# A hybrid DeltaNet and convolution block on one core: results in PSUM emptied by one engine each, and a 31-tap convolution that begins and ends in SBUF

## The chip, the core and the metric

The kernel runs on one core of a Trainium2 chip. The metric is the device time of one execution in microseconds (us). The core's engines, as the profile names them: PE (TensorE, matrix products; PEld is its loading of weights), DVE (VectorE), ACT (ScalarE), POOL (GpSimd) and SP (which here only issues DMAs). Each works through its own list of instructions in order and waits at semaphores for the others. Products land in PSUM, which PE writes and DVE and ACT read; everything else lies in SBUF.

## The reference

One layer, x of 512 tokens by 1024 channels, all in float32:

```python
h = rmsnorm(x, norm1_w)
q, k, v, z, b, a, glu, gates = split(h @ w_in)
q, k, v = silu(causal_depthwise_conv(q | k | v, 4 taps))        # 8 heads of 128
o = gated_delta_rule(l2norm(q), l2norm(k), v, decay(a), sigmoid(b))   # per head, in time
out_a = (rmsnorm(o) * silu(z)) @ dn_w_o
c = glu_a * sigmoid(glu_b)
c = causal_depthwise_conv(c, 31 taps) + cm_dw_b                 # 1024 channels
c = silu(layernorm(c))
out_b = c @ cm_w_pw2 + cm_b_pw2
x = x + (sigmoid(gate_a) * out_a + sigmoid(gate_b) * out_b) @ w_out
x = x + (silu(f_gate) * f_up) @ ffn_w_down                      # f_gate, f_up from rmsnorm(x)
return rmsnorm(x, norm_f_w)
```

The delta rule is S_t = a_t S_(t-1) (I - b_t k_t k_t^T) + b_t k_t v_t^T with o_t = q_t S_t. In chunks it needs the inverse of a unit lower triangular matrix per head and chunk.

## The kernel before

**Products.** Channels lie on the 128 partitions and the 512 tokens along the free axis. Each weight tile (128 x 1024, `raw`) is split into a high part on ACT (`whi`, L111) and a low part on DVE (`wlo`, L112), and a product in full precision is three matmuls: high by high, high by low, low by high (L121). One unit of weights is 24 such matmuls. The weights are loaded three units deep. PE works on these products from beginning to end; everything else is woven between them.

**The mixers**, up to some 475 us of the profile, is the stage that the change touches. A list of generators (`queue`) yields after every three matmuls, and each such step counts one. Besides the products of the projections three other things run there:

- The eight heads' delta rule. `chain(h, ...)` is a generator that says after each piece how many steps are to pass before the next. It builds the inverse of the triangular matrix of 128 x 128 in blocks of 16, 32 and 64: each `group(w, ...)` (L526) is two products into the single PSUM buffer `b`, whose results ACT and DVE carry to their places in `m64`, `Y` (the inverse) and `st64` (shown as `s`). DVE transposes 32 x 32 blocks as it carries them. Then come four state steps, n = 0 to 3, one per 128 tokens, in the single PSUM buffer `st`, which has four slots: slot 0 for k by the state (L622) and later for kd by `w` (L633), slot 2 for q by the state (L623), slot 1 for the inverse by `R` (L628), slot 3 for `at` by `w` (L634). ACT carries slot 1 out as `w` (L630). DVE makes the next state `S` from slot 0 (L640) and the output `o` from slot 3 and from `Ae`, which is slot 2 scaled (L646 and L647; `Ae` lies in a tile named `R`).
- The 31-tap convolution `conv31(i, c)`, eight tiles of 128 channels. ACT makes the first tap into the PSUM tile `cps` (L688), DVE adds 30 more there, one instruction each (L690), ACT copies the result to `cv[i]` in SBUF (L692), and DVE adds it to the running sum `sacc` (L696).
- The four-tap convolutions, the GLU and the gates.

After the last gate PE begins with the output projection of the heads (`yh`, `yl`, split at L878 and L879), and after its first unit of weights PE sums `sacc` over channels for the mean of the layer norm (L709).

**What sets the order.** The kernel is recorded in program order, and a scheduler then orders each engine's instructions by priorities and by its own idea of their times; after that the order is fixed. The taps of `conv31` are recorded with a lower priority (`OFF` = 1600), so they fill the gaps that the scheduler sees on DVE. The chains' steps are pinned behind what was issued last (`behind()`). Where ACT and DVE both read one PSUM buffer, semaphores let them take turns in program order. A product into that buffer waits for the last reader.

Of the kernel before, what the change touches and what calls it, by code (L numbers as in the profile page):

```python
# [6 lines left out]
F32 = mybir.dt.float32  # L7
F32R = mybir.dt.float32r
I32 = mybir.dt.int32
AF = mybir.ActivationFunctionType  # L10
ALU = mybir.AluOpType
# [3 lines left out]
P = 128  # L15
T = 512
# [16 lines left out]
def block_kernel(ctx, tc, a):  # L33
    nc = tc.nc
    V, S, G, PE = nc.vector, nc.scalar, nc.gpsimd, nc.tensor
# [23 lines left out]
    dw_b, ln_w, ln_b, b_pw2 = vec[:, 48:56], vec[:, 56:64], vec[:, 64:72], vec[:, 72:80]  # L59
# [3 lines left out]
    c31w = small.tile([P, KD, 31], F32, name="c31w")  # L63
# [69 lines left out]
    cv = [kp.tile([P, T], F32, name="cv", bufs=KD) for _ in range(KD)]  # L133
# [78 lines left out]
    with tc.tile_pool(name="st", bufs=2) as st:  # L212
# [56 lines left out]
        for k in range(KD):  # L269
# [3 lines left out]
                                   op0=ALU.mult, op1=ALU.subtract)  # L273
            if k % 2 == 0:
                c = slice(k * P, k * P + 256)
# [15 lines left out]
        ps = psg.tile([P, 4, P], F32, name="g")  # L291
# [50 lines left out]
        for k in range(2, 4):  # L342
# [6 lines left out]
                        in1=ss[:, 1].rearrange("p (n a) -> p n a", a=1).broadcast_to([P, NT, 16]), op=ALU.mult)  # L349
# [3 lines left out]
        beta, nbeta, kdf, egc, negc, egl, nmc = (sm[:, i] for i in range(7))  # L353
        ax, t0, sp, u, g, eb = (swt[:, 32 * i:32 * i + 32].rearrange("p (n h) -> p n h", n=NT) for i in range(6))
        V.tensor_tensor(out=ax, in0=bas[:, :, 8:16],
                        in1=rowp[:, 1:2, :].broadcast_to([P, NT, H]), op=ALU.add)
# [172 lines left out]
    def chain(h, kT, qT, ss, kd, b2, Un, cp, Vp, at, yq, zs):  # L529
# [62 lines left out]
            S.copy(out=Y[b, :, b], in_=YY[b])  # L592
        yield 4
        ps = group(32, st32[1], Q)
        S.copy(out=m64[b32[1], :, b32[0]], in_=ps[b32[1]])
        V.transpose(out=m64[b32[3], :, b32[0]], in_=ps[b32[0]])
        S.copy(out=Y[b32[2], od, b32[3]], in_=ps[b32[2]])
        V.transpose(out=Y[b32[2], ev, b32[3]], in_=ps[b32[3]])
        S.copy(out=Y[b32[0], od, b32[1]], in_=ps[b32[0]])
        V.transpose(out=Y[b32[0], ev, b32[1]], in_=ps[b32[1]])  # L600
        S.copy(out=Y[lo64, ev, hi64], in_=Y[hi64, od, hi64])
        yield 5

        ps = group(64, st64[0], m64)
        S.activation(st64[1][hi64, :, hi64], ps[hi64], AF.Copy)
        V.tensor_copy(out=st64[1][lo64, :, lo64], in_=ps[lo64])
        yield 4
        ps = group(64, st64[1], Y[:, ev, hi64])
        S.activation(Y[lo64, ev, hi64], ps[hi64], AF.Copy)
        V.tensor_copy(out=Y[lo64, od, hi64], in_=ps[lo64])  # L610
        yield 3

# [3 lines left out]
        for n in range(NT):  # L616

            ps = pst.tile([P, 4, P], F32, name="st")
            if n == 0:
                R = Vp[:, 0, :]  # L620
            else:
                PE.matmul(ps[:, 0, :], kT[:, n, :], Sp, start=True, stop=True)  # L622
                PE.matmul(ps[:, 2, :], qT[:, n, :], Sp, start=True, stop=True)  # L623
                R = gp.tile([P, P], F32, name="R", bufs=3)
                V.scalar_tensor_tensor(out=R, in0=ps[:, 0, :], scalar=negc[:, n, h:h + 1], in1=Vp[:, n, :],
                                       op0=ALU.mult, op1=ALU.add)
                yield 3
            PE.matmul(ps[:, 1, :], Y[:, n % 2 * 2 + n // 2, :], R, start=True, stop=True)  # L628
            w = gp.tile([P, P], F32, name="w", bufs=2)
            S.activation(w, ps[:, 1, :], AF.Copy, scale=b2[:, n:n + 1])  # L630
            yield 3
            if n < NT - 1:
                PE.matmul(ps[:, 0, :], kd[:, n, :], w, start=True, stop=True)  # L633
            PE.matmul(ps[:, 3, :], at[:, n, :], w, start=True, stop=True)  # L634
            if n < NT - 1:
                Sn = gp.tile([P, P], F32, name="S", bufs=2)
                if n == 0:
                    V.tensor_copy(out=Sn, in_=ps[:, 0, :])
                else:
                    V.scalar_tensor_tensor(out=Sn, in0=Sp, scalar=egl[:, n, h:h + 1], in1=ps[:, 0, :],  # L640
                                           op0=ALU.mult, op1=ALU.add)
            if n == 0:
                V.tensor_copy(out=o[:, 0, :], in_=ps[:, 3, :])
            else:
                Ae = gp.tile([P, P], F32, name="R", bufs=3)
                S.activation(Ae, ps[:, 2, :], AF.Copy, scale=egc[:, n, h:h + 1])  # L646
                V.tensor_tensor(out=o[:, n, :], in0=ps[:, 3, :], in1=Ae, op=ALU.add)  # L647
            S.activation(sq, o[:, n, :], AF.Square, accum_out=ss[:, 2, n:n + 1])
            if n < NT - 1:
                Sp = Sn  # L650
                yield 3
# [33 lines left out]

    def conv31(i, c):
        acc = psc.tile([P, T], F32, name="cps")
        S.activation(acc, c[:, 0:T], AF.Identity, scale=c31w[:, i, 0:1], bias=dw_b[:, i:i + 1])  # L688
        for k in range(1, 31):
            V.scalar_tensor_tensor(out=acc, in0=c[:, k:k + T], scalar=c31w[:, i, k:k + 1], in1=acc,  # L690
                                   op0=ALU.mult, op1=ALU.add)
        S.activation(cv[i], acc, AF.Copy)  # L692
        if i == 1:
            V.tensor_tensor(out=sacc, in0=cv[0], in1=cv[1], op=ALU.add)
        elif i > 1:
            V.tensor_tensor(out=sacc, in0=sacc, in1=cv[i], op=ALU.add)  # L696
# [690 lines left out]
```

## Time and profile before

| what | value |
|---|---|
| median of three runs | 951.15 us (949.65 to 952.15) |
| the profiled execution | 953.04 us, of which the span of the profile is 951.3 us |
| granted PE clock, mean | 0.997 |
| PE busy | 928.8 us, 98% of the span |
| DVE busy | 740.5 us, 78% |
| ACT busy | 560.8 us, 59% |
| POOL busy | 330.7 us, 35% |

A row of the waits' view reads "engine, tile and line <- what ended the wait: total us, times, longest us". A row of a timeline reads "start us, duration us, engine, line, operation, out<-in, shapes, count [idle time before it <- what ended it]". A row of the grouped view has the count, then busy us and mean ns of one, then the idle time before the group and what ended it. The rows of a table by stretches have the stretch, its length, the busy time of PE, PEld, DVE, ACT and POOL with counts, the granted clock, the DMA engines' share and GB/s. Numbers after tile names are left out there (`m<-b` is `m64`, `s` is one of `st16`, `st32`, `st64`).

### The profile page before, as it was taken

How to read it: one execution, taken by the hardware profiler on the slowest of the kernel's cores; microseconds unless marked ns; L12 is line 12 of the kernel's file. 1: busy time of each engine (PE TensorE's matmuls, PEld its weight loads, DVE VectorE, ACT ScalarE, POOL GpSimd, SP SyncE). 2: the span in 40 equal slices, each digit the busy share in tenths (PEclk: the TensorE clock that was granted, in tenths of full speed). 3: DMA queues.
4: the chain of work that ended last, by engine and by line, in shares of the span. 5: the costliest groups of instructions: out<-in, count | busy, mean ns of one | idle time of the engine just before them, and what ended most of it. 6: DMA issues, size and time to landing. Idle time of an engine off the chain costs nothing.

```text
span 951.3 us, 14518 instructions
## 1 busy us (share of the span) xinstructions
PE 928.8 (98%) x4952; PEld 785.9 (83%) x4952; DVE 740.5 (78%) x1157; ACT 560.8 (59%) x1277; POOL 330.7 (35%) x541
## 2 busy tenths in 40 slices
PE   9999999999999999999899999999999999999996
PEld 6778787878887888788778888888889999988885
DVE  4899598888888889899988643676636877888896
ACT  6698887878778786634447323333334454556545
POOL 0045524243443437544034350254441111133042
PEclk9999999999999999999999999999999999999999
DMA  9333322222222236998988983598898555567654
GB/s 321 110 134 104 122 90 78 99 92 68 84 90 87 99 135 148 312 280 268 283 274 253 274 255 131 174 290 285 279 251 233 174 188 187 178 220 253 226 182 150
DMA packets 78187, 177.39 MB, mean 186 GB/s; under 512 B 10080, under 2 KB 19472, under 8 KB 77088
## 3 DMA queue, kind: packets, MB, share of 16 engines
q1 hardware_dynamic: 66528, 144.89, 44.4%
q0 software_dynamic: 10288, 28.90, 13.1%
q10 hardware_dynamic: 1296, 2.67, 0.7%
q8 instruction: 39, 0.64, 0.3%
q14 instruction: 36, 0.29, 0.1%
HBM read 156.22 MB, written 45.37 MB: 212 GB/s over the span
## 4 chain that ended last, share of the span: by engine, by line
PE 70%; ACT 12%; DVE 6%; issue 3%; POOL 3%; DMA 1%; SPq 0%; POOLq 0%; ACTq 0%; DVEq 0%
PE mm L121 44%; PE w L121 20%; ACT whi L111 1%; DVE wlo L112 1%; PE b L526 1%; DVE cps L690 1%; DVE acc L422 1%; DMA sgd<-sg 1%; ACT Y L592 1%; ACT s L583 1%; ACT Un L473 1%; PE g L435 1%; ACT R L646 0%; PE st L628 0%; POOL y L504 0%
## 5 line engine op out<-in xcount | busy, mean ns | idle before, releaser
L111 ACT ACTIVATE whi<-raw 128x1024 fp32r<-128x1024 f32 (+1 forms) x191 | 196.6, 1030 | 250.5 <-PE mm L121 163.6
L112 DVE TENSOR_TENSOR wlo<-raw,whi 128x1024 fp32r<-128x1024 f32 (+1 forms) x191 | 238.0, 1246 | 82.0 <-ACT whi L111 80.2
L121 PE MATMUL mm<-hh,whi 128*128 128x512 f32 (+1 forms) x688 | 268.7, 391 | 0.3 <-ACT hh L336 0.3
L121 PE MATMUL mm<-hl,whi 128*128 128x512 f32 (+1 forms) x688 | 263.3, 383 | 0.0
L121 PE MATMUL mm<-hh,wlo 128*128 128x512 f32 (+1 forms) x688 | 263.1, 383 | 0.0
L690 DVE SCALAR_TENSOR_TENSOR cps<-c,c31w,cps 128x512 f32<-128x512 f32 x240 | 179.8, 749 | 4.2 <-ACT cps L688 0.5
L121 PEld LDWEIGHTS mm<-hh,wlo 128*128 128x128 f32 x688 | 129.6, 188 | 23.2
L121 PEld LDWEIGHTS mm<-hh,whi 128*128 128x128 f32 x688 | 129.9, 189 | 21.3 <-ACT hh L336 0.8
L121 PEld LDWEIGHTS mm<-hl,whi 128*128 128x128 f32 x688 | 130.0, 189 | 20.4
L1020 POOL TENSOR_TENSOR fm<-fm 128x256 f32<-128x256 f32 x33 | 30.6, 929 | 116.0 <-DVE s L1020 93.2
L422 DVE SCALAR_TENSOR_TENSOR acc<-mm,c4w,acc 128x511 f32<-128x511 f32 (+2 forms) x72 | 53.1, 741 | 3.2 <-ACT acc L419 3.0
L502 POOL TENSOR_TENSOR ytm<-U,y 128x60 f32<-128x60 f32 (+14 forms) x120 | 35.3, 294 | 50.2 <-DMA U<-sc 41.4
L196 POOL DMA_DIRECT2D s<-in_wgu_dram x24 | 22.9, 970 | 82.5 <-DMA s<-in_wgu_dram 82.5
L121 PE MATMUL mm<-yh,whi 128*128 128x512 f32 x128 | 51.2, 400 | 0.0
L121 PE MATMUL mm<-yl,whi 128*128 128x512 f32 x128 | 50.0, 391 | 0.0
L121 PE MATMUL mm<-yh,wlo 128*128 128x512 f32 x128 | 49.9, 390 | 0.0
L121 PE MATMUL w<-hh,wlo 128*128 128x256 f32 x168 | 47.7, 284 | 0.4 <-DVE wlo L112 0.4
L121 PE MATMUL w<-hh,whi 128*128 128x256 f32 x168 | 47.6, 284 | 0.0
L121 PE MATMUL w<-hl,whi 128*128 128x256 f32 x168 | 47.5, 283 | 0.0
L121 PE MATMUL w<-wlo,fh 128*128 128x512 f32 (+1 forms) x115 | 44.3, 385 | 0.2 <-DVE wlo L112 0.2
L121 PE MATMUL w<-whi,fl 128*128 128x512 f32 (+1 forms) x115 | 44.2, 385 | 0.0
L121 PE MATMUL w<-whi,fh 128*128 128x512 f32 (+1 forms) x115 | 44.2, 384 | 0.0
(344 smaller groups left out, 1927.9 us busy)
## 6 DMA issues: line engine op xcount, KB each, us to landing
raw<-in_win_dram SPq DMA_DIRECT2D x61, 512.0 KB, 3.3
raw<-in_wgu_dram SPq DMA_DIRECT2D x32, 512.0 KB, 3.4
s<-in_wgu_dram SPq DMA_DIRECT2D x48, 256.0 KB, 5.4
raw<-s SPq DMA_DIRECT2D x48, 256.0 KB, 3.7
raw<-wsum SPq DMA_DIRECT2D x44, 256.0 KB, 3.6
raw<-in_wdn_dram SPq DMA_DIRECT2D x33, 256.0 KB, 3.2
s<-in_wgu_dram POOLq DMA_DIRECT2D x24, 256.0 KB, 6.7
s<-s POOLq DMA_DIRECT2D x24, 256.0 KB, 6.8
```

The source lines that it names most:

```text
L111: marked(S.activation(hi, raw, AF.Copy), "unit")
L112: marked(V.tensor_tensor(out=lo, in0=raw, in1=hi.bitcast(F32), op=ALU.subtract), "unit")
L121: marked(PE.matmul(ps, l, r, start=first and i == 0, stop=last and i == 2))
L196: fed.append(nc.gpsimd.dma_start(*begun.pop(0), accum_op=ALU.add, max_dma_last_dim=2048))
L422: marked(V.scalar_tensor_tensor(out=acc[:, s:], in0=ps[:, :T - s], scalar=c4w[:, j, k:k + 1], in1=acc[:, s:], op0=ALU.mult, op1=ALU.add))
L435: PE.transpose(ps[:, n, :], src[:, n, :], ident)
L473: S.activation(Un[:, n, :], ps[:, n, :], AF.Copy, scale=nb2[:, n:n + 1])
L502: G.tensor_tensor(out=tm[:, :, 0:w], in0=U[:, k, :, k + 1:], in1=y[:, :, k:k + 1].broadcast_to([P, NT, w]), op=ALU.mult)
L526: PE.matmul(ps[:, q, 0:w], stationary[:, q, :], moving[:, q, :], start=True, stop=True)
L583: S.copy(out=st32[1][b, :, b], in_=Ye[b] if i % 2 else Xo[b])
L690: V.scalar_tensor_tensor(out=acc, in0=c[:, k:k + T], scalar=c31w[:, i, k:k + 1], in1=acc, op0=ALU.mult, op1=ALU.add)
L1020: return eng.tensor_tensor(out=out, in0=in0, in1=in1, op=op)
```

## The change

1. After the second product of the 32 group ACT copies the whole result from PSUM into a new SBUF tile `Z` of 128 x 64. The three copies on ACT and the three transposes on DVE then read `Z`.
2. Both halves of the first 64 group's result go out on ACT, both halves of the second on DVE. Before, each had one half on either.
3. In the state steps, `Ae` is made directly behind `w`, one step earlier, and no longer behind `S`.
4. In `conv31` the first tap goes to `cv[i]` instead of `cps`. The second tap reads it there and writes `cps`, the last tap reads `cps` and writes `cv[i]`. The ACT copy at the end is gone.

```diff
         ps = group(32, st32[1], Q)
-        S.copy(out=m64[b32[1], :, b32[0]], in_=ps[b32[1]])
-        V.transpose(out=m64[b32[3], :, b32[0]], in_=ps[b32[0]])
-        S.copy(out=Y[b32[2], od, b32[3]], in_=ps[b32[2]])
-        V.transpose(out=Y[b32[2], ev, b32[3]], in_=ps[b32[3]])
-        S.copy(out=Y[b32[0], od, b32[1]], in_=ps[b32[0]])
-        V.transpose(out=Y[b32[0], ev, b32[1]], in_=ps[b32[1]])
+        Z = gp.tile([P, 2, 32], F32, name="Z")
+        S.activation(Z, ps, AF.Copy)
+        S.copy(out=m64[b32[1], :, b32[0]], in_=Z[b32[1]])
+        V.transpose(out=m64[b32[3], :, b32[0]], in_=Z[b32[0]])
+        S.copy(out=Y[b32[2], od, b32[3]], in_=Z[b32[2]])
+        V.transpose(out=Y[b32[2], ev, b32[3]], in_=Z[b32[3]])
+        S.copy(out=Y[b32[0], od, b32[1]], in_=Z[b32[0]])
+        V.transpose(out=Y[b32[0], ev, b32[1]], in_=Z[b32[1]])
         S.copy(out=Y[lo64, ev, hi64], in_=Y[hi64, od, hi64])
         yield 5
         ps = group(64, st64[0], m64)
         S.activation(st64[1][hi64, :, hi64], ps[hi64], AF.Copy)
-        V.tensor_copy(out=st64[1][lo64, :, lo64], in_=ps[lo64])
+        S.activation(st64[1][lo64, :, lo64], ps[lo64], AF.Copy)
         yield 4
         ps = group(64, st64[1], Y[:, ev, hi64])
-        S.activation(Y[lo64, ev, hi64], ps[hi64], AF.Copy)
+        V.tensor_copy(out=Y[lo64, ev, hi64], in_=ps[hi64])
         V.tensor_copy(out=Y[lo64, od, hi64], in_=ps[lo64])
...
             S.activation(w, ps[:, 1, :], AF.Copy, scale=b2[:, n:n + 1])
+            if n:
+                Ae = gp.tile([P, P], F32, name="R", bufs=3)
+                S.activation(Ae, ps[:, 2, :], AF.Copy, scale=egc[:, n, h:h + 1])
             yield 3
...
             else:
-                Ae = gp.tile([P, P], F32, name="R", bufs=3)
-                S.activation(Ae, ps[:, 2, :], AF.Copy, scale=egc[:, n, h:h + 1])
                 V.tensor_tensor(out=o[:, n, :], in0=ps[:, 3, :], in1=Ae, op=ALU.add)
...
         acc = psc.tile([P, T], F32, name="cps")
-        S.activation(acc, c[:, 0:T], AF.Identity, scale=c31w[:, i, 0:1], bias=dw_b[:, i:i + 1])
+        S.activation(cv[i], c[:, 0:T], AF.Identity, scale=c31w[:, i, 0:1], bias=dw_b[:, i:i + 1])
         for k in range(1, 31):
-            V.scalar_tensor_tensor(out=acc, in0=c[:, k:k + T], scalar=c31w[:, i, k:k + 1], in1=acc,
-                                   op0=ALU.mult, op1=ALU.add)
-        S.activation(cv[i], acc, AF.Copy)
+            V.scalar_tensor_tensor(out=acc if k < 30 else cv[i], in0=c[:, k:k + T], scalar=c31w[:, i, k:k + 1],
+                                   in1=acc if k > 1 else cv[i], op0=ALU.mult, op1=ALU.add)
```

With other dependences the scheduler also orders the rest of the mixers anew. Lines below L596 move down by two, those below `w` by up to five and those of `conv31` by three.

On DVE, at the end of the last convolution, the order before is (L690 are the taps, L696 the sum, `yl` the low part of the heads' output):

```order
L668 SCALAR_TENSOR_TENSOR A<-b,vec,A 128x512
L112 TENSOR_TENSOR wlo<-raw,whi 128x1024
L879 TENSOR_TENSOR yl<-A,yh 128x512 x8
L112 TENSOR_TENSOR wlo<-raw,whi 128x1024
L690 SCALAR_TENSOR_TENSOR cps<-c,c31w,cps 128x512 x4
L893 TENSOR_TENSOR ma<-mm,gsl 128x512
L112 TENSOR_TENSOR wlo<-raw,whi 128x1024
L696 TENSOR_TENSOR sacc<-sacc,cv 128x512
```

and in the changed program:

```order
L693 SCALAR_TENSOR_TENSOR cps<-c,c31w,cps 128x512 x3
L693 SCALAR_TENSOR_TENSOR cv<-c,c31w,cps 128x512
L698 TENSOR_TENSOR sacc<-sacc,cv 128x512
L112 TENSOR_TENSOR wlo<-raw,whi 128x1024 x2
L671 SCALAR_TENSOR_TENSOR A<-b,vec,A 128x512
L112 TENSOR_TENSOR wlo<-raw,whi 128x1024
L881 TENSOR_TENSOR yl<-A,yh 128x512 x8
L112 TENSOR_TENSOR wlo<-raw,whi 128x1024
L895 TENSOR_TENSOR ma<-mm,gsl 128x512
```

The end of the convolution has moved ahead of the last splits of weights, of `A` and of `yl`. Through most of the stage 12 or 13 taps more than before stand ahead of the same weight split.

On DVE, behind the 32 group of the third head, the three transposes before, with the semaphores that they wait for:

```order
L596 STREAM_TRANSPOSE m_468<-b 32x2x32 [waits Activation_49]
L112 TENSOR_TENSOR wlo<-raw,whi 128x1024 [waits DMAHW3_49]
L598 STREAM_TRANSPOSE Y_460<-b 32x2x32 [waits Activation_49]
L112 TENSOR_TENSOR wlo<-raw,whi 128x1024 [waits DMAHW4_49]
L690 SCALAR_TENSOR_TENSOR cps<-c,c31w,cps 128x512 [waits DVE_49]
L600 STREAM_TRANSPOSE Y_460<-b 32x2x32 [waits Activation_49]
```

and in the changed program:

```order
L598 STREAM_TRANSPOSE m_468<-Z 32x2x32 [waits Activation_49]
L600 STREAM_TRANSPOSE Y_460<-Z 32x2x32
L602 STREAM_TRANSPOSE Y_460<-Z 32x2x32
L693 SCALAR_TENSOR_TENSOR cps<-c,c31w,cps 128x512 [waits DVE_49]
L112 TENSOR_TENSOR wlo<-raw,whi 128x1024 [waits DMAHW4_49,Activation_49]
```

The three now stand together and wait for ACT once.

On ACT, in the second state step of the fifth head, `w` and `Ae` (L646, tile `R`) before:

```order
L630 ACTIVATE w<-st,ss 128x128
L550 COPY s_466<-Un 64x2x64
L551 COPY s_466<-Un 64x2x64
L512 ACTIVATE Vp<-g,ss 128x128 x4
L557 ACTIVATE YY<-y,cst 128x4x16
L646 ACTIVATE R<-st,sm 128x128
```

and in the changed program:

```order
L632 ACTIVATE w<-st,ss 128x128
L635 ACTIVATE R<-st,sm 128x128
L550 COPY s_466<-Un 64x2x64
L551 COPY s_466<-Un 64x2x64
L512 ACTIVATE Vp<-g,ss 128x128 x4
L557 ACTIVATE YY<-y,cst 128x4x16
```

`Ae` has moved up to `w`. The semaphore of PE's next product, kd by `w`, which counted up to `w` (L630) before, counts up to `Ae` (L635) now.

## The prediction

> **What bounds the kernel now.** I read the page's busy table first, then TensorE's own waits, then the place of the longest of them on the timelines of the three engines that meet there.
>
> ```profile
> span 951.3 us, 14518 instructions
> PE 928.8 (98%) x4952; PEld 785.9 (83%) x4952; DVE 740.5 (78%) x1157; ACT 560.8 (59%) x1277; POOL 330.7 (35%) x541
> ...
> PEclk9999999999999999999999999999999999999999
> ```
>
> TensorE (PE) is the bound, and the change neither adds nor removes a matmul. So a gain can only come out of PE's waits, of which the view of waits for PE alone shows these as the longest that end on VectorE (DVE) or ScalarE (ACT) work which the diff touches:
>
> ```profile
> PE b L526 <- DVE Y L600: 3.0, 5, 1.0
> PE mm L709 <- DVE sacc L696: 2.8, 1, 2.8
> PE st L622 <- DVE o L647: 1.3, 4, 0.4
> PE b L526 <- POOL y L504: 1.2, 1, 1.2
> PE st L633 <- ACT w L630: 1.0, 2, 0.6
> PE st L622 <- DVE c L678: 0.8, 1, 0.8
> PE st L634 <- ACT w L630: 0.4, 1, 0.4
> ```
>
> The columns are total, times and longest, in us. In all 10.5 us: that is about all there is to win or to lose, beside what hangs on the clock.
>
> **Term 1, the wait for the sum of the long convolution.** The timelines of DVE, ACT and PE, one after the other, just before PE takes `sacc`:
>
> ```profile
> 463.13 4.90 DVE L879 TENSOR_TENSOR yl<-A,yh 128x512 fp32r<-128x512 f32 x8
> 467.95 1.22 DVE L112 TENSOR_TENSOR wlo<-raw,whi 128x1024 fp32r<-128x1024 f32 x1
> 469.08 3.13 DVE L690 SCALAR_TENSOR_TENSOR cps<-c,c31w,cps 128x512 f32<-128x512 f32 x4
> ...
> 473.03 1.23 DVE L112 TENSOR_TENSOR wlo<-raw,whi 128x1024 fp32r<-128x1024 f32 x1 [0.17 <-ACT whi L111]
> 474.17 0.69 DVE L696 TENSOR_TENSOR sacc<-sacc,cv 128x512 f32<-128x512 f32 x1
> ...
> 471.94 1.06 ACT L111 ACTIVATE whi<-raw 128x1024 fp32r<-128x1024 f32 x1 [3.80 <-PE mm L121]
> 472.90 0.58 ACT L692 ACTIVATE cv<-cps 128x512 f32<-128x512 f32 x1
> ...
> 474.91 2.07 PE L709 MATMUL mm<-sacc,cst 128*128 128x512 f32 x2 [2.79 <-DVE sacc L696]
> ```
>
> The last four taps of the last convolution end at 472.2. The copy out of PSUM stands behind a weight split on ACT, the addition behind another on DVE, and PE stands idle for 2.79 us. After that the clock is halved, as the stretches around it show (the column before the DMA share is the granted clock):
>
> ```profile
> 474.40:477.80 3.40, 2.89 (x5) 1.67 (x6) 0.61 (x2) 0.60 (x1) 1.22 (x2) 0.50 1.09 367
> 477.80:485.00 7.20, 7.20 (x34) 5.93 (x32) 7.20 (x9) 3.58 (x6) 5.20 (x6) 1.00 1.03 356
> ```
>
> 3.4 us at 0.50 are 1.7 us of lost matmul time. In the changed order the last tap and `sacc` stand ahead of four weight splits and the eight `yl`: by the rows above 4 x 1.22 + 4.90 = 9.8 us of DVE work, so the sum is ready well before PE asks. This term gives back 2.8 + 1.7 = 4.5 us, and it comes to nothing only if DVE falls 10 us behind. The earlier place comes from idle time that DVE no longer spends waiting for ACT (terms 2 and 3), far less from the copies out of `cps` themselves:
>
> ```profile
> L690 DVE SCALAR_TENSOR_TENSOR cps<-c,c31w,cps 128x512 f32<-128x512 f32 x240 | 179.8, 749 | 4.2 <-ACT cps L688 0.5
> L692 ACT ACTIVATE cv<-cps 128x512 f32<-128x512 f32 x8 | 4.7, 593 | 0.3 <-DVE cps L690 0.3
> L688 ACT ACTIVATE cps<-c,vec,c31w 128x512 f32<-128x512 f32 x8 | 6.3, 783 | 0.1
> ```
>
> The eight copies (L692) are 8 x 0.593 = 4.7 us on ACT, which is idle 41% of the span; seven of them hold up nothing of PE's. The first tap keeps its 0.783 us and the taps their 0.749 us: I take no difference for one operand or result in SBUF. The bounds are plus and minus 0.1 us on 16 taps and 8 activations, 2.4 us spread over 400 us of DVE and ACT time, hidden by the lead of almost 10 us.
>
> The half clock began before PE worked again and ended 3.4 us later; I take it for a result of the idle gap. The Trainium skill ("TensorE: Matmul & The Clock Gate", "Why this matters for your kernels") warns only of idle gaps longer than about 3 us. By that rule a gap of 2.79 us costs no clock, and the term would be 2.8 us and not 4.5; the rows speak for 4.5.
>
> **Term 2, the bank of the 32 and 64 groups.** In the stage of the delta-rule chains the grouped view, with forms kept apart, has one row for the 64-wide group, and the third head shows where its wait comes from (DVE, then PE):
>
> ```profile
> L526 PE MATMUL b<-m,s 128*128 128x64 f32 x32 | 5.0, 277 | 4.3 <-DVE Y L600 3.0 <-POOL y L504 1.2
> ...
> 197.60 0.24 DVE L596 STREAM_TRANSPOSE m<-b 32x64 f32<-32x64 f32 x1
> 197.88 1.23 DVE L112 TENSOR_TENSOR wlo<-raw,whi 128x1024 fp32r<-128x1024 f32 x1
> 199.13 0.26 DVE L598 STREAM_TRANSPOSE Y<-b 32x64 f32<-32x64 f32 x1
> ...
> 201.46 0.24 DVE L600 STREAM_TRANSPOSE Y<-b 32x64 f32<-32x64 f32 x1
> ...
> 195.24 0.53 PE L526 MATMUL b<-Q,s 128*128 128x32 f32 x4
> 201.85 0.63 PE L526 MATMUL b<-m,s 128*128 128x64 f32 x4 [0.97 <-DVE Y L600]
> ...
> 115.65 0.24 DVE L600 STREAM_TRANSPOSE Y<-b 32x64 f32<-32x64 f32 x1
> ```
>
> PE may overwrite the bank only when the last of six readers (L600) is through, and these readers take turns between ACT and DVE, with weight splits in between: 3.86 us from L596 to L600 here. The wait that the page puts down to POOL's `y` (1.2 us) belongs to the same thing, since it ended at 116.04, just behind the L600 at 115.65. Afterwards ACT alone reads the bank, and PE waits for two writers of `m64` instead, the first of the three transposes and the first of the ACT copies. In this head that is L596, done at 197.84 and not at 201.70, plus the new copy into `Z`. Its nearest row is a copy of the same size out of the same bank, L587, at 0.216 us:
>
> ```profile
> L587 ACT ACTIVATE Q<-b 128x64 f32<-128x64 f32 x8 | 1.7, 216 | 0.1
> 433.52 27.24 PE mm L121 x120
> ```
>
> The second row is the longest unbroken piece of matmuls in the chain of waits. `m64` is ready about 2.6 + 0.2 = 2.8 us after the start of PE's 32 group. A big matmul takes 27.24 / 120 = 0.227 us, and the new order leaves 12 to 32 of them in between (before: 15 to 40): 2.7 us in one head, 3.4 us in four, more in three. PE thus still waits a little in some heads, the more so in the two where ACT has a weight's first half (1.06 us, L111 above) between `Z` and the copy. Of the 4.3 us I take back 3.4; the bounds are 4.3 and 0, since the order brings the group closer by up to 14 matmuls.
>
> **Term 3, the state steps.** `Ae` (L646, in the tile `R`) goes ahead. Before, it stood behind DVE's `S` and in front of DVE's `o`, which frees the `st` bank for PE (L622):
>
> ```profile
> L647 DVE TENSOR_TENSOR o<-st,R 128x128 f32<-128x128 f32 x24 | 6.9, 287 | 8.4 <-ACT R L646 8.1
> L646 ACT ACTIVATE R<-st,sm 128x128 f32<-128x128 f32 x24 | 8.8, 366 | 6.2 <-DVE S L640 4.9 <-PE st L634 1.0
> ```
>
> 8.1 us of DVE idle and 4.9 us of ACT idle go; with the four waits and the one that the page gives to a memset (`c`, 0.8) PE loses 2.1 us here now. I take 1.5 of it, the rest staying where `S` itself is late; bounds 2.1 and 0.
>
> Against it stands a new wait. PE's next product (kd by `w`) waited for the evacuation of `w`; in the changed program it waits for `Ae`, one ACT instruction later, 0.366 us by the row above. The weight loads show how often PE already hangs on `w`:
>
> ```profile
> PEld st L633 <- ACT w L630: 3.8, 10, 0.8
> PEld st L634 <- ACT w L630: 1.7, 3, 0.8
> ```
>
> 13 of 32 steps, so at unchanged places 13 x 0.366 = 4.8 us. The order however puts the product up to 5 matmuls later where it was closest (2 to 5 places in the fifth head, 4 to 9 in the first two), and `w` no longer queues behind an `Ae` that waits for DVE. I take a loss of 1.5 us; bounds 4.8 and 0.
>
> **Term 4, the moved copies.** One copy of `s64` goes from DVE to ACT and one of `Y` from ACT to DVE, 0.27 to 0.28 us each way. The first has 15 and more matmuls before it is needed: nothing. The second stands ahead of PE's first state product, and in three heads that product now follows the group at once; DVE can be inside a tap of 0.749 us there, so up to 3 x 0.75 = 2.2 us; the same place cost PE's loads 1.2 us on ACT (4 waits). I take a loss of 0.6; bounds 2.2 and minus 1.2. ACT gets one more table load than before (27 for 26), 1.3 us in a stage where it is busy 66.1 of 85 us (second row of the next fence): nothing.
>
> **The sum.** -4.5 - 3.4 - 1.5 + 1.5 + 0.6 = -7.3 us. Nothing behind the mixers takes it back: from 475 us to the end PE is busy 468.4 of 476.3 us (last row of the next fence), so what starts earlier there ends earlier. The profiled execution has 953.04 us for its span of 951.3 us, which gives 945.7; it lies 1.9 us above the median of 951.15, so on the median I expect 943.9, say 944.
>
> **Rivals.**
> 1. Only the first term is real, and the chains keep their waits in another form: PE gets its 64 group earlier in its own order and waits for `m64`, and the product waits for `Ae` at 13 places. -4.5 - 1.5 - 1.0 + 4.8 + 0.6 = -1.6, about 949.5; 947 to 951 as one or the other bound is reached. For it: the order does shift the 64 group forward by 1 to 14 matmuls in six heads, and `w` is late now. Against it: the waits named L600 end 4 us after the work that is still needed.
> 2. Slower: DVE is overbooked. The new order puts some 12 taps more ahead of the same weight split through most of the stage, 12 x 0.749 = 9 us. The stretches show what room there is (PE, PEld, DVE busy first):
>
> ```profile
> 75.00:130.00 55.00, 52.96 (x270) 43.86 (x269) 42.42 (x73) 46.23 (x126) 26.79 (x71) 1.00 0.33 109
> 130.00:215.00 85.00, 82.13 (x433) 66.59 (x432) 74.30 (x144) 66.14 (x205) 32.58 (x82) 1.00 0.26 88
> ...
> 475.00:951.30 476.30, 468.43 (x2625) 410.79 (x2625) 336.19 (x408) 213.70 (x304) 144.71 (x148) 0.99 0.70 223
> ```
>
> 12.6 + 10.7 = 23 us of idle DVE, much of it between fixed dependences. If a tap stands in front of chain work, PE waits: each head has eight places (three `R`, three `S`, `m64`, `Y`), 64 in all. Half a tap more, 0.37 us, at half of them is 12 us, net +5: 956. It decides from 7.3 / 64 = 0.11 us a place on. Against it: the taps move into idle time that the ping-pong of readers made.
> 3. The half clock after 474 us is not the idle gap's doing, and comes all the same: 1.7 us less, so a gain of 5.6 us: 945.6. For it: the rows show only that the one follows the other; against it: the page's line of granted clocks shows no other dip. The Trainium skill's rule on gaps (the page and section named above) would have it so.
>
> **How the numbers follow.** Forecast (941 to 947) 0.60; rival 1 0.24; rival 2 0.07; rival 3 0.05; more than all bounds, 940 or less, 0.04. About 0.3%, 2.9 us, is what a measurement can tell here: the three runs lie between 949.65 and 952.15. Under 948.3 lie the forecast, rival 3, the 0.04 and half of rival 1: 0.81 faster. The other half of rival 1 and a little of rival 2 are 0.13 within, and 0.06 is left for slower. The range takes in the bounds of the two PE terms and rival 1 up to its middle: 940.5 to 949.5.
>
> **What would show it.** Right: no PE wait for `sacc` and the clock at 1.00 around 470 us; no wait of PE for the third transpose; DVE's idle before `o` gone; `sacc` done ahead of weight splits that it followed. The new wait would read PE `st` waiting for ACT `R`, and term 4 as PE `st` waiting for DVE `Y`. Wrong: the sum of PE's waits between 75 and 475 us still near 10 us under other names, or DVE's taps ahead of `R` and `S` with PE behind them.

## The result and the profile after

The changed kernel takes 943.12 us (median of 4 runs, 942.19 to 944.15) against 951.65 us for the kernel before beside it: ratio 0.9913, 95% interval 0.9895 to 0.9931. A second comparison, made with the experiments, gave 0.9892 (0.9872 to 0.9912). The forecast was 944.0 (940.5 to 949.5). The page of the changed kernel begins:

```profile
span 941.7 us, 14545 instructions
...
PE 925.4 (98%) x4952; PEld 785.3 (83%) x4952; DVE 740.8 (79%) x1157; ACT 558.0 (59%) x1278; POOL 336.8 (36%) x541
```

PE stays the bound. Its waits, from the same view that the prediction began with (total, times, longest):

```profile
PE st L638 <- ACT R L635: 1.2, 2, 0.6
...
PE mm L121 <- DVE wlo L112: 0.8, 1, 0.8
PE mm L121 <- ACT whi L111: 0.8, 2, 0.5
...
PE st L624 <- DVE o L650: 0.7, 1, 0.7
PE b L526 <- ACT m L597: 0.6, 2, 0.4
```

No `sacc`, no third transpose, and about half of the waits for `o`. In their place stand the predicted new wait for `R` (1.2 us) and one that nobody had foreseen, 1.6 us for weight splits (L111, L112). The end of the long convolution on DVE, and the product that uses it on PE:

```profile
444.19 0.75 DVE L693 SCALAR_TENSOR_TENSOR cv<-c,c31w,cps 128x512 f32<-128x512 f32 x1
444.97 0.69 DVE L698 TENSOR_TENSOR sacc<-sacc,cv 128x512 f32<-128x512 f32 x1
...
457.91 4.89 DVE L881 TENSOR_TENSOR yl<-A,yh 128x512 fp32r<-128x512 f32 x8
...
466.81 1.02 PE L711 MATMUL mm<-sacc,cst 128*128 128x512 f32 x2
```

`sacc` is ready at 445.7, 21 us before PE takes it; before, it was 2.79 us late. The granted clock stays whole there (the figure ahead of the last two):

```profile
465.00:480.00 15.00, 15.00 (x66) 1.00 1.01 345
```

The groups of the chains, the state steps and the taps, with forms kept apart (busy, mean ns, idle before and its cause):

```profile
L526 PE MATMUL b<-m,s 128*128 128x64 f32 x32 | 4.7, 268 | 0.6 <-ACT m L597 0.6
L650 DVE TENSOR_TENSOR o<-st,R 128x128 f32<-128x128 f32 x24 | 6.8, 285 | 0.7 <-PE st L639 0.6
L693 DVE SCALAR_TENSOR_TENSOR cps<-c,c31w,cps 128x512 f32<-128x512 f32 x224 | 167.9, 749 | 3.8
L693 DVE SCALAR_TENSOR_TENSOR cps<-c,c31w,cv 128x512 f32<-128x512 f32 x8 | 7.8, 979 | 0.1
L693 DVE SCALAR_TENSOR_TENSOR cv<-c,c31w,cps 128x512 f32<-128x512 f32 x8 | 5.9, 742 | 0.1
```

The 64 group waits 0.6 us in place of 4.3, and DVE's idle time ahead of `o` falls from 8.4 to 0.7 us. The fourth row is a surprise: the second tap, the one with both operands in SBUF, takes 0.979 us in the mean against 0.749 for a tap that accumulates in PSUM. That mean is not one price: five of the eight take 0.73 to 0.75 us, the other three 0.97, 1.22 and 1.93.

From 75 to 475 us, the stretch that the prediction named for its sign of being wrong, PE's idle time falls from 11.6 to 4.5 us, so the waits have not come back under other names.

**The unforeseen stall.** Early in the first head PE now waits three times within 3 us, and in this profile the clock is halved afterwards. Its timeline, then the granted clock:

```profile
73.33 0.50 PE L121 MATMUL mm<-hh,whi 128*128 128x512 f32 x1 [0.34 <-ACT whi L111]
...
74.54 0.50 PE L121 MATMUL mm<-hh,whi 128*128 128x512 f32 x1 [0.47 <-ACT whi L111]
...
76.10 0.79 PE L121 MATMUL mm<-hh,wlo 128*128 128x512 f32 x1 [0.82 <-DVE wlo L112]
```

```profile
76.00:77.00 1.00, 0.90 (x2) 0.50 0.00 0
77.00:78.00 1.00, 1.00 (x4) 0.50 0.93 299
...
79.00:80.00 1.00, 1.00 (x6) 0.84 0.93 246
```

The cause stands in the order of ACT. Before, the seventh split of a weight (`whi`, L111) stood behind `kd`; now two first taps (L691), which need no PSUM tile any longer, stand ahead of `kd`, and the split has moved far back: it starts 16.9 us after the sixth (72.22 against 55.34), where it started 3.6 us after it (60.21 against 56.58). The order from the sixth split on, before:

```
L111 ACTIVATE whi<-raw 128x1024
L457 ACTIVATE pa,ss<-g 128x128 x3
L460 ACTIVATE kd<-g,sm 128x128 x3
L111 ACTIVATE whi<-raw 128x1024
L449 ACT_TABLE_LOAD
```

and now, where the next split comes 13 rows behind the last of these:

```
L111 ACTIVATE whi<-raw 128x1024
L457 ACTIVATE pa,ss<-g 128x128
L691 ACTIVATE cv<-c,vec,c31w 128x512
L457 ACTIVATE pa,ss<-g 128x128
L691 ACTIVATE cv<-c,vec,c31w 128x512
L457 ACTIVATE pa,ss<-g 128x128
L460 ACTIVATE kd<-g,sm 128x128 x2
L449 ACT_TABLE_LOAD
```

### The profile page after: what moved, and what is told of

Its sections match the earlier page's. It is cut to its first block, busy times and chain, and to the rows that moved or that the text cites. A ratio compares the mean times of both kernels' runs of the same rounds, so it can differ in the third digit from the quotient of the medians.

```text
span 941.7 us, 14545 instructions
## 1 busy us (share of the span) xinstructions
PE 925.4 (98%) x4952; PEld 785.3 (83%) x4952; DVE 740.8 (79%) x1157; ACT 558.0 (59%) x1278; POOL 336.8 (36%) x541
## 4 chain that ended last, share of the span: by engine, by line
PE 82%; ACT 7%; DVE 3%; issue 1%; POOL 1%; DMA 1%; POOLq 0%; ACTq 0%; DVEq 0%; SPq 0%
PE mm L121 55%; PE w L121 20%; PE b L526 2%; DVE wlo L112 1%; ACT whi L111 1%; PE g L435 1%; PE g L470 1%; PE st L639 1%; PE st L630 1%; PE st L638 1%; PE st L624 1%; PE st L625 0%; ACT Un L473 0%; DVE xs L964 0%; PE b L435 0%
## 5 line engine op out<-in xcount | busy, mean ns | idle before, releaser
L111 ACT ACTIVATE whi<-raw 128x1024 fp32r<-128x1024 f32 (+1 forms) x191 | 196.4, 1030 | 242.6 <-PE mm L121 158.0
L112 DVE TENSOR_TENSOR wlo<-raw,whi 128x1024 fp32r<-128x1024 f32 (+1 forms) x191 | 239.6, 1256 | 86.1 <-ACT whi L111 84.8
L693 DVE SCALAR_TENSOR_TENSOR cps<-c,c31w,cps 128x512 f32<-128x512 f32 x224 | 167.9, 749 | 3.8
L1022 POOL TENSOR_TENSOR fm<-fm 128x256 f32<-128x256 f32 x33 | 28.1, 852 | 117.7 <-DVE s L1022 93.2
```

Source lines behind the costliest of these rows:

```text
L111: marked(S.activation(hi, raw, AF.Copy), "unit")
L112: marked(V.tensor_tensor(out=lo, in0=raw, in1=hi.bitcast(F32), op=ALU.subtract), "unit")
L693: V.scalar_tensor_tensor(out=acc if k < 30 else cv[i], in0=c[:, k:k + T], scalar=c31w[:, i, k:k + 1], in1=acc if k > 1 else cv[i], op0=ALU ...
L1022: return eng.tensor_tensor(out=out, in0=in0, in1=in1, op=op)
```

## The experiments

All were timed against the kernel before.

| Kernel | What it holds | Ratio, 95% interval |
|---|---|---|
| conv | the convolution's edit alone | 0.9958 (0.9946 to 0.9970) |
| chain | groups and `Ae`, old convolution | 0.9944 (0.9932 to 0.9957) |
| banks | groups alone | 0.9944 (0.9927 to 0.9962) |
| zonly | `Z` alone | 0.9974 (0.9961 to 0.9986) |
| g64 | the 64 groups' copies alone | 1.0001 (0.9989 to 1.0013) |
| ae | `Ae` ahead alone | 1.0183 (1.0167 to 1.0200) |
| noae | changed, `Ae` in its old place | 0.9927 (0.9913 to 0.9940) |
| mix1 | changed, first of the first taps in PSUM | 0.9907 (0.9894 to 0.9921) |
| psumtap | changed, all first taps in PSUM | 0.9892 (0.9874 to 0.9910) |
| psnoae | psumtap, `Ae` in its old place | 0.9921 (0.9906 to 0.9935) |
| sbufacc | changed, all taps accumulate in SBUF | 1.0197 (1.0177 to 1.0216) |
| changed, again | as it is | 0.9892 (0.9872 to 0.9912) |

### The parts by themselves: conv and chain

conv takes from the diff only its last part, with the change of the taps' targets between these lines; chain takes all but that.

```
-        S.activation(acc, c[:, 0:T], AF.Identity, scale=c31w[:, i, 0:1], bias=dw_b[:, i:i + 1])
+        S.activation(cv[i], c[:, 0:T], AF.Identity, scale=c31w[:, i, 0:1], bias=dw_b[:, i:i + 1])
...
-        S.activation(cv[i], acc, AF.Copy)
```

> Only the long convolution's edit: first tap into cv, last tap into cv, no copy; the chains as before. Theory A: the early place of sacc comes from this edit (its taps stand up to 13 places ahead in DVE's order with the chains as before, and the sum stands ahead of 5 more weight splits), and so does a new early stall at 73 to 79 us (1.6 us of PE waits for weight splits and then half clock for 3.4 us, 1.7 us): no PE wait for sacc, no dip at 474 us, a dip near 76 us; -4.5 + 3.3 = -1.2 us against before, ratio 0.9985 to 0.9990. Theory B, as the prediction had it: the earlier place comes from DVE idle time that the other parts free, so alone this edit leaves the wait for sacc of 2 us or more and the dip after it: 0 to +3.3 us, ratio 1.000 to 1.0035.

> Only the chains' edits (Z, s64, Y, Ae); the long convolution as before. Theory A: the chains are worth 8.5 - 1.2 = 7.3 us and sacc is still late: PE waits over 1 us for it, the clock is halved after it, no stall near 75 us; ratio 0.9920 to 0.9930. Theory B: freed idle time of DVE brings sacc early as well: no wait for sacc, 4.5 us more, -11.8 us, ratio 0.9875.

conv gave 947.06 us beside 951.19, a gain of 4.1. There is no wait for `sacc` and no dip at 470 us, so theory A has the place right, but its size was missed (1.2 us): the third of the early waits is absent in this kernel and so is the half clock. chain gave 946.24, a gain of 5.0, with `sacc` as late as ever. Theory A again, but less than its 7.3. The two gains add up to 9.1 us; the change had 8.5 and 10.3 in its two comparisons. Now the end of the convolution in chain, on DVE, ACT and PE:

```profile
466.04 1.22 DVE L112 TENSOR_TENSOR wlo<-raw,whi 128x1024 fp32r<-128x1024 f32 x1 [0.17 <-ACT whi L111]
467.18 0.68 DVE L699 TENSOR_TENSOR sacc<-sacc,cv 128x512 f32<-128x512 f32 x1
...
464.95 1.06 ACT L111 ACTIVATE whi<-raw 128x1024 fp32r<-128x1024 f32 x1 [3.80 <-PE mm L121]
465.91 0.58 ACT L695 ACTIVATE cv<-cps 128x512 f32<-128x512 f32 x1
...
467.92 1.13 PE L712 MATMUL mm<-sacc,cst 128*128 128x512 f32 x2 [2.78 <-DVE sacc L699]
```

DVE's idle time ahead of `o` is down from 8.4 to 2.4 us in this kernel,

```profile
L650 DVE TENSOR_TENSOR o<-st,R 128x128 f32<-128x128 f32 x24 | 6.8, 284 | 2.4 <-PE st L639 2.4
```

and yet the wait is the same to 0.01 us. The rows say why. The wait is a loop that PE itself starts: a split (`whi`) had waited 3.80 us for PE to release its buffer; the copy of `cv` stands behind that split on ACT, `sacc` behind its second half on DVE, and PE behind `sacc`. However early the taps are done, split, second half and sum come after PE's own matmul. The copy itself is through at 466.49 and the sum starts at 467.18, behind the second half; what counts is the place of the sum in DVE's order.

### Which half of the convolution's edit does it: psumtap and mix1

psumtap is the changed kernel with the first tap in PSUM; mix1 does the same for the first of the eight convolutions only (`t0 = acc if i < 1 else cv[i]`).

```
-        S.activation(cv[i], c[:, 0:T], AF.Identity, scale=c31w[:, i, 0:1], bias=dw_b[:, i:i + 1])
+        S.activation(acc, c[:, 0:T], AF.Identity, scale=c31w[:, i, 0:1], bias=dw_b[:, i:i + 1])
...
-                                   in1=acc if k > 1 else cv[i], op0=ALU.mult, op1=ALU.add)
+                                   in1=acc, op0=ALU.mult, op1=ALU.add)
```

> The changed kernel, but the first of the eight convolutions keeps its first tap in PSUM (its last tap still writes cv, no copy). In the order the second convolution's first tap then no longer stands ahead of the seventh weight's split on ACT, and sacc still has no weight split or yl between it and the last tap. Theory A: the stall at 73 to 76 us and the half clock after it go, 1.6 + 1.7 = 3.3 us: 939.8, ratio to before 0.9875. Rival: the stall is not due to that order, or another wait takes its place in the next matmuls: 943, ratio 0.991. If the half clock needs the stall, the granted clock of 75 to 80 us is 1.00 here and 0.6 or so in the changed kernel.

> The changed kernel with the first tap of all eight convolutions back in PSUM; the last tap still writes cv and there is no copy. So of the convolution's edit only the second half is left. In DVE's order the last tap now stands ahead of three weight splits and the eight yl, but sacc behind two and the yl. Theory A: the first tap's new home is what brought sacc forward (and the early stall); here the wait for sacc is between 0 and 2 us, no stall near 75 us, no second tap over 0.80 us; with the run that changed only one convolution at 0.9907 this is 0.9905 to 0.994. Theory B: the missing copy is what counts, since the wait for sacc began with it: no wait, as fast as the best run, 0.989 to 0.9905. If the half clock hangs on the length of the gap, a gap below 2 us shows a clock of 1.00 behind it.

psumtap took 941.42 us, the changed kernel beside it 941.76: theory B. The copy's absence alone ends the wait, as its DVE and PE rows show:

```profile
452.85 0.75 DVE L693 SCALAR_TENSOR_TENSOR cv<-c,c31w,cps 128x512 f32<-128x512 f32 x1
...
460.17 1.22 DVE L112 TENSOR_TENSOR wlo<-raw,whi 128x1024 fp32r<-128x1024 f32 x1
461.31 0.69 DVE L698 TENSOR_TENSOR sacc<-sacc,cv 128x512 f32<-128x512 f32 x1
...
464.26 1.02 PE L711 MATMUL mm<-sacc,cst 128*128 128x512 f32 x2
```

`sacc` now stands one split further ahead and is ready 2.3 us early. chain and psumtap differ in nothing but this copy and the last tap's target, and their ratios by 0.0052, 4.9 us (0.0022 to 0.0083 if both intervals are taken at their ends): the prediction's 4.5.

So the first tap's new home brought 19 us more of lead that nobody needed, and the early stall. In mix1 and psumtap that stall is gone (no wait for L111 or L112 near 75 us), but neither beats the changed kernel: mix1 took 942.16, 0.9907 against 0.9913 and 0.9892. Theory A's 3.3 us for mix1 was too much. That the stall hangs on the places of the first taps on ACT is shown, since it goes with them; that its 1.6 us, which stand in both profiles of the changed kernel, cost the kernel as much is not. mix1 has a wait of 1.3 us for `o` and waits of 1.9 us for `R` in its profile, more than the changed kernel's 0.7 and 1.2.

### The state steps: noae, psnoae, ae

noae and psnoae put `Ae` back, in the changed kernel and in psumtap; ae makes the reverse edit in the kernel before.

```
-            if n:
-                Ae = gp.tile([P, P], F32, name="R", bufs=3)
-                S.activation(Ae, ps[:, 2, :], AF.Copy, scale=egc[:, n, h:h + 1])
...
+                Ae = gp.tile([P, P], F32, name="R", bufs=3)
+                S.activation(Ae, ps[:, 2, :], AF.Copy, scale=egc[:, n, h:h + 1])
                 V.tensor_tensor(out=o[:, n, :], in0=ps[:, 3, :], in1=Ae, op=ALU.add)
```

> The changed kernel with Ae back in its old place (behind DVE's S). Theory A (the prediction's term 3): Ae ahead gives back about 1.5 us of waits and costs about as much in the new wait of kd times w, so this kernel is within 1.5 us of the changed one, 943 to 944.5, ratio to before 0.991 to 0.9925; DVE's idle before o (8 us) is back and the PE waits for R in L638 (1.2 us) are gone. Rival: the idle that Ae frees on DVE carries the chains' gain: 3 us or more are lost, 946 to 948, ratio 0.9945 to 0.996. Second rival: the new wait is the larger side, 941 to 942, ratio 0.989 to 0.990.

> The kernel with all first taps in PSUM and no copy, and Ae back behind S. Theory A: the net of Ae ahead is nothing, as with and without it beside the groups' edits (0.9944 both): ratio 0.989 to 0.9905; the waits for R in L638 and L639 go and those for o and w come, sums within 1 us. Rival: Ae ahead is worth 1 us or more where the rest of the chains is clean: 0.9908 or more. sacc has no wait if its place in the order decides, since that is the same with and without Ae.

> Only Ae goes ahead; all else as before. In DVE's order the last twelve taps of the long convolution now stand behind one more weight split and the eight yl, where before it was the last four. Theory A: the place in the order decides; sacc comes later by up to 8 taps x 0.75 - 1.2 = 4.8 us, PE waits 4 to 8 us for it and the clock is halved after it for 3.4 us or longer; the waits of the state steps give nothing in the sum: 951 to 956, ratio 1.000 to 1.005. Theory B, as the prediction had it: the idle time that goes on DVE (8 us) brings sacc forward by itself: its wait is 2 us or less, and with 1.5 us of the waits for o the ratio is 0.994 to 0.998.

noae took 944.35 us, within theory A's 943 to 944.5. Against the changed kernel's 0.9913 and 0.9892 its 0.9927 is 1.3 to 3.3 us more. psnoae lies 2.8 us above psumtap (0.0029), which speaks for its rival. But chain and banks, which differ by the same edit, have the same ratio. `Ae` ahead is thus worth 0 to 3 us, more than the prediction's nothing, and the intervals do not say more.

Alone, it is a disaster: 968.18 us, 17 us slower. The waits of PE in this kernel, then DVE's last taps:

```profile
PE mm L710 <- DVE sacc L697: 16.5, 1, 16.5
PE mm L121 <- ACT whi L111: 4.9, 1, 4.9
```

```profile
474.64 12.63 DVE L691 SCALAR_TENSOR_TENSOR cps<-c,c31w,cps 128x512 f32<-128x512 f32 x16
487.93 0.69 DVE L697 TENSOR_TENSOR sacc<-sacc,cv 128x512 f32<-128x512 f32 x1 [0.66 <-ACT cv L693]
```

The copies are the same and the idle time of DVE ahead of `o` is gone here too (1.3 us), but the scheduler gave the taps later places: 20 of them stand behind the eight `yl`, where theory A had counted twelve and the kernel before has four, and the last 16 stand behind the last split, in PE's path. The 4.9 us are another matter of order, on ACT: at 188 to 193 us a split stands behind a long row of the chains' copies. Theory A had the mechanism and a third of its size; theory B, the prediction's reason, has the wrong sign.

### The groups: banks, zonly, g64

banks makes all edits of the groups, zonly only the copy into `Z` with its six readers, g64 only the two exchanged copies:

```
-        V.tensor_copy(out=st64[1][lo64, :, lo64], in_=ps[lo64])
+        S.activation(st64[1][lo64, :, lo64], ps[lo64], AF.Copy)
...
-        S.activation(Y[lo64, ev, hi64], ps[hi64], AF.Copy)
+        V.tensor_copy(out=Y[lo64, ev, hi64], in_=ps[hi64])
```

> Only the groups' edits (Z, s64, the two copies of Y); Ae and the convolution as before. Theory A (the prediction's terms 2 and 4): these carry the chains' gain, so of the 5.0 us that all of the chains' edits gave about 3.4 to 4 are here, 947.2 to 947.8, ratio 0.9955 to 0.9965; the waits named L600 are gone, the waits for DVE's o and ACT's w stay. Rival: Ae carries it, and the groups only move their wait (PE waits for m64): -1.5 us or less, ratio 0.9985 or more. Since sacc is late in all kernels with the old first tap, its wait of over 2 us and the half clock should stand here too.

> Only the bank of the 32 group: ACT copies it into Z, and the six later copies read Z. The copies of the 64 groups, Ae and the convolution stay as before. Theory A (the prediction's term 2): the 4.3 us of PE waits behind the third transpose are its doing; -3.4 us, ratio 0.9955 to 0.9975, no PE wait for L600. Rival: the 5 us that all groups' edits gave come as much from the 64 groups, where one engine in place of two empties the bank: then -2 us or less here, ratio 0.998 or more. sacc late by 2.8 us with the half clock behind it, as in every kernel with the old convolution.

> The other half of the groups' edits: one copy of the first 64 group goes to ACT, one of the second to DVE, so that each bank is emptied by one engine; no Z. Theory A (the prediction's term 4): no gain, +0.6 us, ratio 0.999 to 1.002, and the waits for L600 stand as before. Rival: the two readers of a bank that took turns cost PE; without the turns -1.5 to -2.5 us, ratio 0.9975 to 0.9985, and DVE's or ACT's idle time before these copies is smaller by 1 us or more in the sum of eight heads.

`Z` alone gives 2.5 us (1.3 to 3.7) and g64 nothing (within 1.2 us either way). In g64 that is theory A, and the rival's gain lies outside the interval; in zonly the middle is theory A's, but the interval reaches into the rival's 2 us or less. Beside each other they gave 5.3 us (3.6 to 6.9) in banks, against 3.4 to 4 by theory A there; the intervals leave open whether that is more than the sum. In zonly no PE wait for L600 is left, but part of the gain moved to other waits:

```profile
PE st L624 <- DVE o L649: 2.9, 5, 1.2
PE mm L711 <- DVE sacc L698: 2.8, 1, 2.8
PE st L635 <- ACT w L632: 1.5, 3, 0.7
```

The waits for `o` were 1.3 us before and those for `w` at that place 1.0; here they are 2.9 and 1.5, and in banks 1.2 and 0.6. Each of these is one profile.

The 1.2 us that the view puts down to POOL's `y` are gone in zonly, banks and chain and are still there in g64 and ae, which have no `Z`. The prediction was right to count them to the bank.

### Two operands in SBUF: sbufacc

```
-            V.scalar_tensor_tensor(out=acc if k < 30 else cv[i], in0=c[:, k:k + T], scalar=c31w[:, i, k:k + 1],
-                                   in1=acc if k > 1 else cv[i], op0=ALU.mult, op1=ALU.add)
+            V.scalar_tensor_tensor(out=cv[i], in0=c[:, k:k + T], scalar=c31w[:, i, k:k + 1],
+                                   in1=cv[i], op0=ALU.mult, op1=ALU.add)
```

> The changed kernel with all 30 taps in SBUF (accumulating in cv, no PSUM tile): a dose of two SBUF operands, 240 times in place of 8. In the runs so far such a tap took 0.75 us where POOL was idle or busy with some of its work, and 0.97 to 1.9 us where it met POOL's U, Un or cp. Theory A: it is a contention with POOL, so the mean lies between 0.78 and 0.95 us with single taps over 1.2, not one new price; 240 x 0.1 = 24 us more DVE work in some 400 us, against about 60 us of idle time: the prediction's rival 2 in a strong dose. If idle time takes it, 0.991 to 0.995; if half of it is seen by PE, 12 us, ratio 1.004. Theory B: the operands in SBUF cost a fixed 0.25 us each: all taps near 1.0 us, 60 us more DVE work, ratio 1.03 or more. POOL's own spans should grow too under A.

970.71 us, 19 us slower than before and 29 slower than the changed kernel beside it. Both theories were wrong on the time: the mean tap is A's, the loss is not. The taps, then POOL's work:

```profile
L692 DVE SCALAR_TENSOR_TENSOR cv<-c,c31w,cv 128x512 f32<-128x512 f32 x240 | 189.7, 818 | 1.3
```

```profile
L504 POOL TENSOR_TENSOR y<-y,ytm 128x60 f32<-128x60 f32 (+14 forms) x120 | 61.7, 514 | 9.4
L502 POOL TENSOR_TENSOR ytm<-U,y 128x60 f32<-128x60 f32 (+14 forms) x120 | 55.0, 459 | 51.8 <-DMA U<-sc 43.0
...
L481 POOL COPY cp<-Un 32x128 f32<-32x128 f32 x28 | 16.8, 598 | 1.3
```

In the changed kernel the same three are:

```profile
L504 POOL TENSOR_TENSOR y<-y,ytm 128x60 f32<-128x60 f32 (+14 forms) x120 | 38.3, 319 | 9.4
L502 POOL TENSOR_TENSOR ytm<-U,y 128x60 f32<-128x60 f32 (+14 forms) x120 | 36.7, 306 | 51.0 <-DMA U<-sc 42.2
...
L481 POOL COPY cp<-Un 32x128 f32<-32x128 f32 x28 | 9.3, 333 | 1.3
```

Against the changed kernel DVE's busy time for the 240 taps grows by 8 us (from 167.9 + 7.8 + 5.9 = 181.6), POOL's by 49 us on these three lines. POOL's 120 steps of the delta rule's substitution are a serial chain at the head of each group, and PE waits where it comes late:

```profile
PE g L435 <- ACT kT L425: 6.1, 2, 5.2
PE b L526 <- ACT Q L571: 5.4, 1, 5.4
```

ACT's `kT` of the first row ended a chain that ran back, over two more operations of POOL (`ss` and `DT`), to `y` and `ytm` from 153 to 170 us. In all PE is idle for 34.5 us of the span here (967.4 less 932.9) and for 16.3 in the changed kernel (941.7 less 925.4). This is the prediction's rival 2, taps that make the chains late, in a strong dose, and it comes through POOL.

### The half clock: the changed kernel again

No edit; the same kernel once more.

> The changed kernel again, to have it on the same chip as the others. If the half clock behind the three short waits near 75 us is a matter of chance, as the run with Ae in its old place hints (the same three waits of 0.35, 0.47 and 0.80 us and a clock of 1.00), this profile can show the dip or not, and its time is 941.5 to 944; if it belongs to this kernel, the dip of 3.4 us is there again.

The same three waits were there, and this time the clock did not fall:

```profile
73.36 0.49 PE L121 MATMUL mm<-hh,whi 128*128 128x512 f32 x1 [0.32 <-ACT whi L111]
...
74.56 0.50 PE L121 MATMUL mm<-hh,whi 128*128 128x512 f32 x1 [0.47 <-ACT whi L111]
...
76.13 0.50 PE L121 MATMUL mm<-hh,wlo 128*128 128x512 f32 x1 [0.83 <-DVE wlo L112]
```

```profile
77.00:78.00 1.00, 1.00 (x6) 1.00 0.90 238
```

It did not in noae either, with waits of 0.35, 0.47 and 0.80 us. So the same three short waits went with a half clock in one profile of three, and in the same kernel once and once not. What decides it is not shown.

## Why the prediction was right, and where it was not

The time, the direction and the size are those of the likeliest case: -8.5 us measured, -7.3 forecast. The waits named are the ones that went, but the close total is in part luck: term 1 had its size for a wrong reason, an unforeseen stall stands against term 4's loss, which did not come, and whatever term 3 gave, and some of the gain lies where the sum did not look (last point). Step by step:

- **Term 1, 4.5 us: the size right, the reason wrong.** Removing the wait for `sacc` gave 4.9 us (chain against psumtap). The step that failed is "The earlier place comes from idle time that DVE no longer spends waiting for ACT (terms 2 and 3), far less from the copies out of `cps` themselves". Idle time moved nothing (chain: wait unchanged at 2.78 us) and `Ae` alone made the wait 16.5 us; the copy's absence moved the sum, by changing the order. That the size came out all the same is luck. The clock's share was read a little high: in the 3.4 us at 0.50 the row has PE busy for 2.89, which is 1.4 us of lost matmul time and not 1.7. The step "I take no difference for one operand or result in SBUF" holds for the result (0.742 us); a second tap, with two operands there, took as much as any other in five cases of eight and up to 1.93 us beside POOL's work. That is 1.8 us of DVE time in all, and no row of PE's waits names a second tap. The lead is 21 us, not 10, and 19 of these come from the first tap's home.
- **Rival 3, that the half clock was not the gap's doing: refuted.** All five kernels with a gap of 2.78 to 2.79 us before `sacc` (before, chain, banks, zonly, g64) show a mean clock of 0.89 from 465 to 480 us, all others but ae, whose gap is 16.5 us, show 1.00. The page's line of granted clocks, used as an argument here, could not decide it: it has a 9 even in the slices of the dip. The Trainium skill's rule ("TensorE: Matmul & The Clock Gate", "Why this matters for your kernels": idle gaps over about 3 us) is too generous here: 2.78 us was enough each time.
- **Term 2, 3.4 us:** 2.5 measured for `Z` alone (1.3 to 3.7). The wait at the 64 group fell by 3.7 us as predicted, but in zonly about 2 us came back as waits for `o` and `w`.
- **Term 3, net 0:** 0 to 3 us gained. The new wait for `Ae` is 1.2 us in PE and 3.5 us in its weight loads, near the 1.5 taken; the gain, taken at 1.5, was if anything too small.
- **Term 4, 0.6 us lost:** nothing (g64 1.0001, within 1.2 us).
- **Left out, the stall:** that a first tap without a PSUM tile may go ahead of a weight split on ACT. PE waits 1.6 us for it, and in one profile of three the clock was halved for 3.4 us behind it; mix1 and psumtap, which have no stall, are not faster than the changed kernel.
- **Left out, what the view of waits does not hold:** "a gain can only come out of PE's waits". Between the two profiles PE's idle time falls by 6.2 us (from 951.3 less 928.8 to 941.7 less 925.4). The other 3.4 us of the 9.6 are busy time, for the same 4952 matmuls at the same mean clock of 0.997. In a row of big matmuls each record lasts 0.39 us though the next starts 0.23 us after it, so a stop can hide some 0.16 us in busy time; that this is where the 3.4 us went is an estimate, not shown.

## What to carry to other kernels

Where an order is planned, an edit's price is not that of its instructions but that of the places it moves: `Ae` alone cost 17 us, beside the other edits it gave up to 3. Look for a wait that loops back to the waiting engine (here PE, weight buffer, split, its second half, sum, PE): it has the same length whatever idle time is won elsewhere, and only another place or a removed link ends it. Before an accumulator is moved from PSUM to SBUF, see what GpSimd does at that time and who waits for it.

## What was not expected of the hardware

A DVE operation with two SBUF operands and POOL's work stretch each other. In the changed kernel second taps took from 0.73 to 1.93 us; the two longest, 1.93 and 1.22, ran beside POOL's sums of weights (`U`). In sbufacc the effect is on the other side: six taps in a row, then POOL's steps at that time:

```profile
166.79 4.05 DVE L692 SCALAR_TENSOR_TENSOR cv<-c,c31w,cv 128x512 f32<-128x512 f32 x6
```

```profile
167.67 0.58 POOL L502 TENSOR_TENSOR ytm<-U,y 128x8 f32<-128x8 f32 x1
168.33 0.59 POOL L504 TENSOR_TENSOR y<-y,ytm 128x8 f32<-128x8 f32 x1
168.99 0.58 POOL L502 TENSOR_TENSOR ytm<-U,y 128x4 f32<-128x4 f32 x1
```

The steps start every 0.66 us, one for each tap of 4.05 / 6 = 0.675 us. In the changed kernel steps of 16 to 8 elements from 157.13 to 158.32 us, beside taps that accumulate in PSUM, took 0.22 us and started every 0.30 us. The taps themselves are not dearer by nature: the median of the 240 is 0.745 us. The Trainium skill ("SBUF — State Buffer", "SBUF: two separate sides") has it that GpSimd and a DVE operation with two SBUF inputs share a pair of ports by an exclusive lock, held for the whole instruction; the rows agree, in both directions.

Between 1.6 and 2.8 us of idleness these runs saw the clock do either: it did not fall behind 2.0 us (sbufacc at 393 to 396 us, PE busy 0.96 of 3 us, clock 1.00 after), fell in one of three profiles behind three waits of 1.6 us in all, and five times of five behind 2.78 us. The fall does not mark the gap. In the kernel before it came at 474.4 us, with PE still idle; in chain the gap ended at 467.92 us, the clock was 1.00 up to 469 us and 0.50 from 469.5 us on.
